# A hand-scheduled section emitted directly instead of in a block with one program per engine

## The chip, the cores and the metric

One core of a Trainium2 chip. The metric is the device time of one execution in microseconds (us). A profiled execution has a "span", from its first to its last recorded instruction, which is about 1.8 us shorter than the device time here. Every run of this study carries the state "fast": its granted clock, a share of full speed that the profile gives, is 1.0. A few of them are nevertheless 40 to 48 us (0.8 to 1.0%) longer than the others of the same kernel. Below they are called outlying runs, and the experiments ended up being largely about them.

## The reference

```python
# x: (256, 256, 4096) float32, eps = 1e-5
mean = np.mean(x, axis=2, keepdims=True)
var = np.var(x, axis=2, keepdims=True)
return ((x - mean) / np.sqrt(var + eps)).astype(np.float32)
```

## The kernel before

The input is taken as 128 tiles of 8.39 MB, each of 128 partitions with four rows of 4096 values. Three tile buffers go round: SyncE (S) loads and stores, VectorE (V) sums and normalises, ScalarE (A) makes the sums of squares and normalises three quarters of one row in four. All synchronisation is by hand, with semaphores: `take` waits for a count and clears the semaphore.

```python
def take(engine, sem, count):
    engine.wait_ge(sem, count)
    engine.sem_clear(sem)

def store(s, t):
    take(S, done[s], K + 1)
    S.dma_start(out=rows_of(out_t, t), in_=X[s][:, :, :]).then_inc(stored[s], 16)

def load(s, t, wait=True):
    if wait:
        take(S, stored[s], 16)
    S.dma_start(out=X[s][:, :, :], in_=rows_of(x_t, t)).then_inc(loaded[s], 16)

with tc.tile_critical():            # the framework adds no synchronisation inside
    with nc.Block() as block:       # a program per engine; a barrier at its end
        @block.sync
        def _(sync):
            ...                     # first loads and stores
            with S.Fori(0, rounds) as i:          # 41 rounds of 3 tiles
                for t in range(L0, L0 + BUFS):
                    store(t % BUFS, (t, BUFS, rounds, i))
                    load((t + 2) % BUFS, (t + 2, BUFS, rounds, i))
            ...                     # last loads and stores, waits for the last stores
        @block.vector
        def _(vector):
            ...
            with V.Fori(0, rounds) as i:
                for j in range(BUFS):
                    vector_tile((L0 + j) % BUFS)
            ...
        @block.scalar
        def _(scalar):
            ...                     # the same with A and scalar_tile
```

## Time and profile before

| kernel before | |
|---|---|
| median of 3 runs | 4962.77 us (4962.52 to 4963.97) |
| span, instructions | 4960.0 us, 5954 |
| data moved, mean rate | 2147.5 MB, 433 GB/s |
| busy: VectorE, ScalarE | 66%, 49% |
| mean time from store to store, 30th to 60th store | 38.638 us |

### The profile page before, as it was taken

What the parts mean: (1) busy time and instruction counts of PE and PEld (TensorE: products, weight loads), DVE (VectorE), ACT (ScalarE), POOL (GpSimd) and SP (SyncE); (2) the same over time, 40 slices, a digit from 0 to 9 for tenths busy, and PEclk for the clock granted to TensorE, in tenths of its full rate; (3) what the DMA queues carried; (4) which work ended last, traced back from release to release, by engine and by line L of the source; (5) the groups of instructions that cost most, each with busy time, mean ns of one, the idle gap of its engine ahead of it and who ended that gap; (6) DMA issues with size and microseconds to landing.
All of it is one profiled execution on the core that took longest, in us unless ns stands there. A gap on an engine that the chain in (4) does not pass through costs nothing.

```text
span 4960.0 us, 5954 instructions
## 1 busy us (share of the span) xinstructions
DVE 3298.0 (66%) x2049; ACT 2407.6 (49%) x1412; POOL 0.2 (0%) x4
## 2 busy tenths in 40 slices
DVE  6666666666666666666666666666666666666666
ACT  4454444554445544455445544455444554445544
POOL 0000000000000000000000000000000000000000
DMA  9999999999999999999999999999999999999999
GB/s 423 431 437 432 431 437 432 432 438 433 434 435 432 435 434 432 436 434 432 436 434 432 437 433 432 438 433 432 438 432 434 435 433 435 434 432 436 434 432 403
DMA packets 37298, 2147.52 MB, mean 433 GB/s; under 512 B 4144, under 2 KB 4144, under 8 KB 4144
## 3 DMA queue, kind: packets, MB, share of 16 engines
q1 hardware_dynamic: 37296, 2147.50, 100.0%
q14 instruction: 2, 0.02, 0.0%
HBM read 1073.74 MB, written 1073.74 MB: 433 GB/s over the span
## 4 chain that ended last, share of the span: by engine, by line
DVE 62%; another core or an unknown queue 31%; issue 4%; DMA 2%; ACT 0%; DVEq 0%; ACTq 0%; SPq 0%
DVE x L87 44%; DVE x L112 17%; DMA x<-in_x_dram 1%; DVE nbias L100 1%; DMA out_dram<-x 1%; DVE rstd L98 1%; ACT junk L137 0%; DVEq L68 0%; DVEq L225 0%; ACT L146 0%; ACT std L146 0%; DVEq L193 0%; ACTq L68 0%; ACTq L67 0%
## 5 line engine op out<-in xcount | busy, mean ns | idle before, releaser
L87 DVE TENSOR_SCALAR_CACHE_REDUCE x<-x 128x4096 f32<-128x4096 f32 x512 | 2232.3, 4416 | 1579.9 <-DMA x<-in_x_dram 1579.9
L137 ACT ACTIVATE junk<-x,mean 128x4096 f32<-128x4096 f32 x512 | 1883.1, 3678 | 2366.7 <-DVE x L87 2366.7
L112 DVE TENSOR_SCALAR x<-x,rstd,nbias 128x4096 f32<-128x4096 f32 (+1 forms) x512 | 1004.2, 2004 | 33.9 <-DVE nbias L100 29.3
L151 ACT ACTIVATE x<-x,nbias,rstd 128x3072 f32<-128x3072 f32 x130 | 383.2, 2948 | 146.2 <-DVEq L68 146.2
L137 ACT ACTIVATION_READ_ACCUMULATOR junk<-x,mean 128x1 f32 x512 | 95.5, 186 | 0.0
L146 ACT ACTIVATE std<-ss,eps_tile 128x2 f32<-128x2 f32 x256 | 75.6, 295 | 19.1
L98 DVE RECIPROCAL rstd<-std 128x2 f32<-128x2 f32 x256 | 40.7, 159 | 19.4 <-ACT std L146 19.4
L100 DVE SCALAR_TENSOR_TENSOR nbias<-mean,rstd 128x2 f32<-128x2 f32 x256 | 41.1, 161 | 8.9
L87 DVE DVE_READ_ACCUMULATOR x<-x 128x1 f32 x512 | 42.4, 83 | 0.0
L137 ACT ACT_TABLE_LOAD x1 | 1.3, 1283 | 1.2 <-DVE eps_tile L222 1.2
L146 ACT ACT_TABLE_LOAD x1 | 1.3, 1283 | 0.1
L222 DVE MEMSET eps_tile<- 128x1 f32 x1 | 0.1, 59 | 1.0 <-SPq L192 1.0
L259 POOL MEMSET const-bfloat16-1.0<- 128x1 bf16 x1 | 0.1, 103 | 0.0
L259 POOL MEMSET const-uint8-127<- 128x1 uint8 x1 | 0.1, 101 | 0.0
L259 POOL MEMSET const-float32-0.0<- 128x1 f32 x1 | 0.1, 99 | 0.2 <-issue 0.2
L259 POOL MEMSET const-float32-1.0<- 128x1 f32 x1 | 0.1, 98 | 0.0
## 6 DMA issues: line engine op xcount, KB each, us to landing
out_dram<-x SPq DMA_DIRECT2D x4, 4096.0 KB, 19.4
x<-in_x_dram SPq DMA_DIRECT2D x2, 4096.0 KB, 16.8
x<-in_x_dram SPq DMA_DIRECT2D x127, 50.3
out_dram<-x SPq DMA_DIRECT2D x126, 31.5
```

Source lines behind the costliest of these rows:

```text
L87: V.tensor_scalar(out=x[:, r, :], in0=x[:, r, :], scalar1=1.0 / d, scalar2=None, op0=ALU.mult, op1=ALU.add, accum_out=mean[s][:, r : r + 1 ...
L98: mine(V.reciprocal(out=rstd[s][:, c], in_=std[s][:, c]))
L100: mine(V.scalar_tensor_tensor(out=nbias[s][:, c], in0=mean[s][:, c], scalar=-1.0 / d, in1=rstd[s][:, c], op0=ALU.mult, op1=ALU.mult))
L112: V.tensor_scalar(out=x[:, r, f], in0=x[:, r, f], scalar1=rstd[s][:, c], scalar2=nbias[s][:, c], op0=ALU.mult, op1=ALU.add,).then_inc(dn, 1)
L137: mine(A.activation(out=junk, in_=x[:, r, :], func=AF.Square, bias=mean[s][:, c], scale=-float(d), accum_out=ss[s][:, c]))
L146: A.activation(out=std[s][:, c], in_=ss[s][:, c], func=AF.Sqrt, bias=eps_tile, scale=1.0 / d**3).then_inc(stds, 1)
L151: A.activation(out=x[:, last, :Q], in_=x[:, last, :Q], func=AF.Identity, bias=nbias[s][:, c], scale=rstd[s][:, c]).then_inc(dn, 1)
L222: V.memset(eps_tile, eps / d**2).then_inc(ready, 1)
L259: nc = _bacc.Bacc("TRN2", target_bir_lowering=False, num_devices=1)
```

## The change

The section keeps its outer frame and loses the block. The calls of the three engines now stand one after another in the source, in the order SyncE, VectorE, ScalarE, and each call goes to its own engine's stream. The intent is to be rid of the block's branches and of its exit barrier. Cut to its core:

```diff
     with tc.tile_critical():
-        with nc.Block() as block:
-
-            @block.sync
-            def _(sync):
-                for h in range(2):
-                    ...
-                with S.Fori(0, rounds) as i:
-                    ...
-            @block.vector
-            def _(vector):
-                V.memset(eps_tile, eps / d**2).then_inc(ready, 1)
-                ...
-            @block.scalar
-            def _(scalar):
-                take(A, ready, 1)
-                ...
+        for h in range(2):
+            ...
+        with S.Fori(0, rounds) as i:
+            ...
+        V.memset(eps_tile, eps / d**2).then_inc(ready, 1)
+        ...
+        take(A, ready, 1)
+        ...
```

(The bodies are the same lines, only less indented.)

More of the change, by code (lines that the diff above doesn't have):

```diff
@@ L192 @@
     with tc.tile_critical():
-        with nc.Block() as block:
-            @block.sync
-            def _(sync):
-                for h in range(2):
-                    r = half_of(h)
-                    S.dma_start(out=X[0][:, r, :], in_=x_t[0][:, r, :]).then_inc(second(loaded, 0, h), 16)
-                load(1, 1, wait=False)
-                store_half(0, 0, 0)
-                store_half(0, 0, 1)
-                load(2, 2, wait=False)
-                store(1, 1)
-                take(S, stored[BUFS], 16)
-                load(0, 3)
-                with S.Fori(0, rounds) as i:
-                    for t in range(L0, L0 + BUFS):
-                        store(t % BUFS, (t, BUFS, rounds, i))
-                        load((t + 2) % BUFS, (t + 2, BUFS, rounds, i))
-                load(last % BUFS, last)
-                store((last - 2) % BUFS, last - 2)
-                store((last - 1) % BUFS, last - 1)
-                store_half(last % BUFS, last, 0)
-                store_half(last % BUFS, last, 1)
-                for s in ((last - 2) % BUFS, (last - 1) % BUFS, last % BUFS, BUFS):
-                    take(S, stored[s], 16)
-            @block.vector
-            def _(vector):
-                V.memset(eps_tile, eps / d**2).then_inc(ready, 1)
-                halves(vector_tile, 0, True)
-                vector_tile(1)
-                with V.Fori(0, rounds) as i:
-                    for j in range(BUFS):
-                        vector_tile((L0 + j) % BUFS)
-                vector_tile((last - 2) % BUFS)
-                vector_tile((last - 1) % BUFS)
-                halves(vector_tile, last % BUFS, False)
-            @block.scalar
-            def _(scalar):
-                take(A, ready, 1)
-                halves(scalar_tile, 0, True)
-                scalar_tile(1)
-                with A.Fori(0, rounds) as i:
-                    for j in range(BUFS):
-                        scalar_tile((L0 + j) % BUFS)
-                scalar_tile((last - 2) % BUFS)
-                scalar_tile((last - 1) % BUFS)
-                halves(scalar_tile, last % BUFS, False)
@@ new lines @@
+        for h in range(2):
+            r = half_of(h)
+            S.dma_start(out=X[0][:, r, :], in_=x_t[0][:, r, :]).then_inc(second(loaded, 0, h), 16)
+        load(1, 1, wait=False)
+        store_half(0, 0, 0)
+        store_half(0, 0, 1)
+        load(2, 2, wait=False)
+        store(1, 1)
+        take(S, stored[BUFS], 16)
+        load(0, 3)
+        with S.Fori(0, rounds) as i:
+            for t in range(L0, L0 + BUFS):
+                store(t % BUFS, (t, BUFS, rounds, i))
+                load((t + 2) % BUFS, (t + 2, BUFS, rounds, i))
@@ new lines @@
+        load(last % BUFS, last)
+        store((last - 2) % BUFS, last - 2)
+        store((last - 1) % BUFS, last - 1)
+        store_half(last % BUFS, last, 0)
+        store_half(last % BUFS, last, 1)
+        for s in ((last - 2) % BUFS, (last - 1) % BUFS, last % BUFS, BUFS):
+            take(S, stored[s], 16)
+        V.memset(eps_tile, eps / d**2).then_inc(ready, 1)
+        halves(vector_tile, 0, True)
+        vector_tile(1)
+        with V.Fori(0, rounds) as i:
+            for j in range(BUFS):
+                vector_tile((L0 + j) % BUFS)
@@ L246 @@
+        vector_tile((last - 2) % BUFS)
+        vector_tile((last - 1) % BUFS)
+        halves(vector_tile, last % BUFS, False)
+        take(A, ready, 1)
+        halves(scalar_tile, 0, True)
+        scalar_tile(1)
+        with A.Fori(0, rounds) as i:
+            for j in range(BUFS):
+                scalar_tile((L0 + j) % BUFS)
+        scalar_tile((last - 2) % BUFS)
+        scalar_tile((last - 1) % BUFS)
+        halves(scalar_tile, last % BUFS, False)
 _INS = ['x', 'eps']
```

## The prediction

The forecast's sum is 0.03 + 0.19 + 0.06 = 0.28 us, from 4962.77 to 4962.5 us.

> **What bounds the kernel now.** I began with the profile's page, to see which resource is full. Its first two parts give the busy shares of the engines and of the 16 DMA engines, slice by slice, and its third part gives the DMA queues (packets, MB, share of the DMA engines' time).
>
> ```profile
> span 4960.0 us, 5954 instructions
> DVE 3298.0 (66%) x2049; ACT 2407.6 (49%) x1412; POOL 0.2 (0%) x4
> ...
> DMA  9999999999999999999999999999999999999999
> ...
> DMA packets 37298, 2147.52 MB, mean 433 GB/s; under 512 B 4144, under 2 KB 4144, under 8 KB 4144
> ...
> q1 hardware_dynamic: 37296, 2147.50, 100.0%
> q14 instruction: 2, 0.02, 0.0%
> ```
>
> The DMA row is full in all 40 slices, while VectorE works two thirds of the time and ScalarE half. The bytes are the input once and the output once (2 x 1073.74 MB), so none can be saved: 2147.52 MB at 433 GB/s is 4960 us, the whole span. The second queue is instruction fetch: two packets in the whole run, which I use below.
>
> A full DMA row says that queues are occupied, not that nothing delays them. So I next read one loop tile in the timeline (start, duration, engine, line, what; idle time and its releaser in brackets).
>
> ```profile
> 2406.69 4.42 DVE L87 TENSOR_SCALAR_CACHE_REDUCE x<-x 128x4096 f32<-128x4096 f32 x1 [12.55 <-DMA x<-in_x_dram]
> ...
> 2433.13 0.34 SPq L165 DMA_DIRECT2D out_dram<-x  x1
> 2433.71 0.35 SPq L170 DMA_DIRECT2D x<-in_x_dram  x1
> 2445.34 4.42 DVE L87 TENSOR_SCALAR_CACHE_REDUCE x<-x 128x4096 f32<-128x4096 f32 x1 [12.45 <-DMA x<-in_x_dram]
> ...
> 2471.64 0.34 SPq L165 DMA_DIRECT2D out_dram<-x  x1
> 2472.22 0.35 SPq L170 DMA_DIRECT2D x<-in_x_dram  x1
> 2483.98 4.42 DVE L87 TENSOR_SCALAR_CACHE_REDUCE x<-x 128x4096 f32<-128x4096 f32 x1 [12.56 <-DMA x<-in_x_dram]
> ```
>
> A tile takes 2483.98 - 2445.34 = 38.64 us. It moves 2 x 8.389 MB = 16.78 MB, which is 434 GB/s. VectorE finishes and then waits about 12.5 us for the next load. When the store is issued at 2433.13, the previous load is still arriving; its first reader starts only at 2445.34. So about 12 us of work lies in the DMA queue when new work is added: SyncE could be that much late before the queue ran dry. A delay of less than that in compute or in issuing, once per tile, should cost nothing.
>
> The change concerns the edges of the program, so I then read who waited for whom on SyncE in the last 10 us (engine, line, releaser: total us, times, longest), and the instructions of the line that opens the block (duration in ns, first and last start in us).
>
> ```profile
> SPq L68 <- DMA out_dram<-x: 9.6, 1, 9.6
> SPq L273 <- PEq L273: 0.5, 2, 0.4
> SPq L193 <- PEq L193: 0.2, 1, 0.2
> ...
> L193 POOLq DRAIN  x1: 41/41/41, 0.9 to 0.9; - x1
> L193 PEldq DRAIN  x1: 8/8/8, 1.0 to 1.0; - x1
> ...
> L193 SPq DRAIN  x1: 7/7/7, 4958.8 to 4958.8; - x1
> L193 SPq EVENT_SEMAPHORE  x1: 17/17/17, 4958.9 to 4958.9; - x1
> ```
>
> The last half store is issued at 4941.19 and lands 17.5 us later, at 4958.7. SyncE clears its semaphore, then enters the block's exit barrier at 4958.8 and leaves it about 0.2 us later; PE's release is the last to come, at 0.2 us. Everything after the last landing takes 4960.0 - 4958.7 = 1.3 us, most of it in barriers that the change does not touch (the section's own exit and the program's two end barriers). PE and POOL wait in the block's exit barrier from the first microsecond on, since they have no program in it; VectorE and ScalarE join it near 4941. Only SyncE's arrival is on the path.
>
> [...] the loops' compare-and-branch has a median of 45 ns on SyncE and 56 ns on VectorE. [...] The trace shows two instruction packets in 4960 us with 41 loop-backs on each of three engines[...]. [...] SyncE's 7 ns drain and 17 ns semaphore in the block's exit span about 0.2 us, so I cost the barrier from start to start and not by adding durations.
>
> **The change part by part.** A comparison of the two built programs, engine by engine and with the semaphores that each waits for, shows that all DMAs, all VectorE and ScalarE instructions, their sizes, order, loops and semaphore counts are the same. The three parts stand one after another in the source, but each engine still gets a stream of its own. What differs is this.
>
> First, each working engine loses its branch from the section into its own program. On SyncE this lies ahead of the first load, but the trace records no instruction for it: from the end of the section's entry branch (0.84 us) to the first load (0.96 us) is 0.12 us in all, so it may already have become a plain fall-through. I take 0.03 us from a possible 0 to 0.1.
>
> Second, the block's exit barrier goes: five drains and six semaphore instructions, which I count in the rows of that line. Only SyncE's passage is on the path: from the drain at about 4958.78 to SyncE's next instruction at about 4958.97, so 0.19 us.
>
> Third, PE and POOL have no work left in the section, so the section's entry and exit no longer include them: two branches with a wait at the start, two drains at the end, and one of SyncE's three semaphore waits (successive ones start about 0.05 us apart). This exit collects the slowest engine, and PE is the last to drain there (about 4959.1); without it I take 0.06 us.
>
> The sum is 0.03 + 0.19 + 0.06 = 0.28 us. The loop, 38.64 us times the tiles, is untouched. From 4962.77 this makes 4962.5 us, or 0.006%. The recorded instructions should fall by 11 + 2 + 2 + 1 = 16, from 5954 to about 5938.
>
> **The rivals.** (a) Another barrier takes over the whole saving: the section's exit still synchronises SyncE, VectorE and ScalarE after the last store. For it speaks that the program's end barrier, too, is released by PE (0.5 us). Against it, barriers here follow each other in series, and PE and POOL will now stand at the end barrier long before SyncE. It would make 4962.8. (b) The loops' code moves[...]. For it: addresses do shift. Against it: the streams only lose a few instructions, two packets were fetched before, and about 12 us per tile would hide such a stall. It would make 4962 to 4964 while hidden[...]. (c) The engines run one part after another, as the source now reads. That would be far slower or would hang, as SyncE's part waits for VectorE's; equal waits and separate streams speak against it. (d) The DMA pace falls differently, because loads and stores overlap at another phase. For it: 1% of pace is 50 us. Against it: every slice is full, and the steady tile repeats to 0.01 us after a start-up that the change does not reorder. (e) The block delayed the start by much more than I think. But the first load goes out at 0.96 us in all, most of it in the program's own preamble, so at most some tenths are to be had: 4962.2.
>
> **Range and chances.** The effect is smaller than the spread of the three runs (4962.52 to 4963.97, 1.45 us). The range has to hold that spread[...]: 4958 to 4967. A change beyond 2% is 99 us, or 0.77 us in each of the 128 tiles after the 12 us of slack is used up[...]. [...] I give 0.5% to faster, 98.5% to same and 1% to slower.
>
> **What would show it.** In the changed profile: the same 434 GB/s and 38.64 us per tile; VectorE still idle about 12.5 us before each tile's first pass; the first load at about 0.93 us; no line of the block, and the stretch from the last store's landing to the end at 1.0 to 1.1 us instead of 1.3; two packets of instruction fetch; about 5938 instructions. I would be wrong if the tile period moved by more than 0.05 us (6 us over the run), if instruction packets multiplied, or if VectorE's wait before a tile shrank because its own stream had slowed.

## The result, and the profile after

The changed kernel took 4961.92 us (median of 6 runs, 4961.67 to 4962.52), the kernel before 4962.85 us in its six (4961.47 to 4963.97). Ratios here are the mean time of one kernel's runs over that of the other's of the same rounds, so not quite the ratio of these medians. The ratio is 0.9998, with a 95% interval of 0.9986 to 1.0011: the same, inside the predicted range.

The page of the changed kernel, to be held against the page lines in the prediction:

```profile
span 4960.2 us, 5938 instructions
DVE 3298.0 (66%) x2049; ACT 2407.7 (49%) x1412; POOL 0.2 (0%) x4
...
DMA packets 37298, 2147.52 MB, mean 433 GB/s; under 512 B 4144, under 2 KB 4144, under 8 KB 4144
...
q14 instruction: 2, 0.02, 0.0%
```

16 instructions fewer, as counted; the compute and the bytes are equal. One loop tile in the timeline of the changed kernel (start, duration, engine, line, what):

```profile
2434.53 0.34 SPq L165 DMA_DIRECT2D out_dram<-x  x1
2435.11 0.35 SPq L170 DMA_DIRECT2D x<-in_x_dram  x1
2446.75 4.42 DVE L87 TENSOR_SCALAR_CACHE_REDUCE x<-x 128x4096 f32<-128x4096 f32 x1 [12.46 <-DMA x<-in_x_dram]
...
2485.37 4.42 DVE L87 TENSOR_SCALAR_CACHE_REDUCE x<-x 128x4096 f32<-128x4096 f32 x1 [12.54 <-DMA x<-in_x_dram]
```

2485.37 - 2446.75 = 38.62 us, and the same 12.5 us of waiting for each load. Store to store, the 30th to the 60th are 38.638 us apart on average, to the digit as before. The loop was not touched.

At the head, the first load in the timeline of before and then of after:

```profile
0.96 0.86 SPq L199 DMA_DIRECT2D x<-in_x_dram  x2
```

```profile
0.96 0.86 SPq L195 DMA_DIRECT2D x<-in_x_dram  x2
```

Nothing was gained there. At the tail, the section's exit sits on the line that opens the section. First SyncE's rows of it in the kernel before (count, durations in ns, first and last start), then in the kernel after:

```profile
L192 SPq EVENT_SEMAPHORE  x3: 17/28/28, 4959.0 to 4959.2; - x3
L192 SPq NOP  x2: 13/13/13, 0.7 to 4959.3; - x2
```

```profile
L192 SPq NOP  x2: 13/13/13, 0.7 to 4959.4; - x2
L192 SPq EVENT_SEMAPHORE  x2: 17/22/28, 4959.2 to 4959.4; - x2
```

The starts, read from the traces' own time stamps to the nanosecond: before, SyncE enters the block's barrier at 4958.756, starts the section's exit at 4958.969, starts the no-operation that closes it at 4959.256, and the span ends at 4960.044. After, the exit starts at 4959.227, its no-operation at 4959.442, and the span ends at 4960.202. So the block's barrier took 0.21 us and is gone, the section's exit went from 0.29 to 0.21 us, and the rest from 0.79 to 0.76 us. From SyncE's first such instruction to the end, 1.29 us became 0.98 us: 0.31 us saved. (Expectation e0 below says 1.24 us, which was worked out with the span rounded to 4960.0.) In these two executions the whole span did not become shorter, because the last half store was issued at 4941.68 instead of 4941.19. This half microsecond is scatter in the loop. Held store against store, the changed kernel is 1.4 us behind from the 31st store on, after another start-up, and wins back 0.9 us late: loads arrive every 38.638 us and then, to the end, every 38.72 us, and this step comes at 4068 us before and at 4494 us after. The step is also in the normal traces with fifty barriers below (at 4146 and 3699 us), and not in that of the second copy; what it comes from is not shown.

### The profile page after: what moved, and what is told of

It reads as the page before. It is cut to its first block, busy times and chain, and to the rows that moved or that the text cites. A ratio compares the mean times of both kernels' runs of the same rounds, so it can differ in the third digit from the quotient of the medians.

```text
span 4960.2 us, 5938 instructions
## 1 busy us (share of the span) xinstructions
DVE 3298.0 (66%) x2049; ACT 2407.7 (49%) x1412; POOL 0.2 (0%) x4
## 4 chain that ended last, share of the span: by engine, by line
DVE 62%; another core or an unknown queue 31%; issue 4%; DMA 2%; ACT 0%; DVEq 0%; ACTq 0%; SPq 0%
DVE x L87 44%; DVE x L112 17%; DMA x<-in_x_dram 1%; DVE nbias L100 1%; DMA out_dram<-x 1%; DVE rstd L98 1%; ACT junk L137 0%; DVEq L68 0%; DVEq L219 0%; ACT L146 0%; ACT std L146 0%; ACTq L68 0%; ACTq L67 0%; SPq L265 0%
## 5 line engine op out<-in xcount | busy, mean ns | idle before, releaser
L98 DVE RECIPROCAL rstd<-std 128x2 f32<-128x2 f32 x256 | 40.7, 159 | 19.4 <-ACT std L146 19.4
```

The source lines that it names most:

```text
L98: mine(V.reciprocal(out=rstd[s][:, c], in_=std[s][:, c]))
```

## The experiments

Twelve kernels ran, in four sets. Every set has its own runs of the kernel before, on the same chip. Where means without outlying runs are given, runs above 4970 us are left out; the unedited ratio is given too.

### The changed kernel again

> The changed kernel once more, in five rounds against the kernel before. My theory (one barrier of about 0.2 us and a thinner section exit of about 0.1 us, both once per run): 0.3 us faster, ratio 0.99994, and the stretch from SyncE's last semaphore clear to the end of the span about 1.0 us instead of 1.24 us. Rival, the block cost nothing on the path: ratio 1.0000 and 1.24 us. Rival, the DMA pace changed with the block: a ratio off by 0.001 or more and another tile period than 38.64 us.

Median 4961.86 us against 4962.31 us; ratio 0.9982, interval 0.9945 to 1.0018. The interval is this wide because one of the 7 runs took 5003.43 us and two of the 11 runs of the kernel before took 5001.73 and 5008.59 us. Without those three, the means are 4961.80 and 4962.17 us, 0.37 us apart; in the first measurement the means were 0.78 us apart. Both have the predicted sign, and neither resolves 0.3 us, as runs of one kernel spread by 2 us. The traces do resolve it. The profiled run was the outlying one, but its tail is the same: 0.975 us from SyncE's first instruction of the section's exit to the end, as in the first trace of the changed kernel. In the eight later traces in which the changed exit stands alone, with extra passes, written-out loops or no computation ahead of it, it is 0.970 to 0.982 us. The 1.29 us of the kernel before come from one trace. The outlying run also gave the first view of the other state:

```profile
1500.00:2400.00 900.00, 595.90 (x369) 433.83 (x255) 0.00 (x0) 1.00 1.00 430
2700.00:3600.00 900.00, 594.82 (x371) 432.44 (x254) 0.00 (x0) 1.00 1.00 429
```

These are stretches of that run (window, its length, busy time with instruction counts of VectorE, ScalarE and GpSimd, clock, DMA share, GB/s). In the same windows the normal run of the changed kernel has:

```profile
1500.00:2400.00 900.00, 599.80 (x374) 436.58 (x257) 0.00 (x0) 1.00 1.00 434
2700.00:3600.00 900.00, 597.55 (x373) 434.35 (x255) 0.00 (x0) 1.00 1.00 434
```

The DMA share is 1.00 in both, and the rate differs by 1%. Store to store, the normal runs of the two kernels settle after some 30 tiles into a pattern of three (38.50, 38.57, 38.84 us; late in the run 38.60, 38.65, 38.92), while the outlying run wanders between 38.5 and 40.2 us (mean 39.08) to its end. I call the first the steady rhythm. Only this one outlying run was profiled; that the others are of the same kind is taken from their times. Both kernels have outlying runs: over all sets 3 of 44 runs before and 1 of 13 after, which says nothing about a difference between them.

### Fifty barriers at the end, and fifty at the start

```diff
         halves(scalar_tile, last % BUFS, False)
+        for _ in range(50):
+            with nc.Block() as block:
+                pass
```

The second kernel has the same three lines as the first statement of the section, ahead of the first load.

> The changed kernel with 50 empty blocks, each with its exit barrier over all engines, behind the last wait of the section: the suspected cost multiplied by 50 at the end. My theory: every barrier there is on the path and costs 0.2 to 0.4 us (0.21 us is what one took in the kernel before; back to back each also waits for PE), so 10 to 20 us longer than the changed kernel. Rival, barriers at the end are absorbed by the program's own end: 0 to 1 us. The loop should be untouched: 434 GB/s and 38.64 us per tile.

> The same 50 empty blocks ahead of the first load instead of at the end. My theory: the first load goes out 10 to 20 us later and the whole run is longer by just that, because a DMA-bound run has no slack that could win back a late start. Rival, the start is hidden (for instance by time that VectorE waits for loads anyway): the run is longer by under 3 us.

At the end: 4979.29 us (ratio 1.0036, interval 0.9990 to 1.0083, one run of 6 outlying at 5026.89). At the start: 4979.23 us (ratio 1.0017, interval 0.9981 to 1.0054, none outlying). Against the changed kernel's 4961.86 us of the same set both are 17.4 us longer, or 0.35 us for each block, inside the expected 10 to 20 us. Both rivals (under 1 us, under 3 us) fall. In the trace with the barriers at the start, the first load goes out at 18.31 us instead of 0.96 us:

```profile
18.31 0.86 SPq L198 DMA_DIRECT2D x<-in_x_dram  x2
```

(18.31 - 0.96) / 50 = 0.347 us. The two views agree, so a block's exit barrier is paid in full on either side, and neither the slack of the loop nor the end of the program takes any of it back. In the two traces 44 and 43 of the 49 steps from one barrier to the next take 0.33 us. Three and four are clearly longer (0.52 to 0.82 us), each within 0.8 us ahead of one of the four more instruction packets that these longer streams fetch, and they add about 1.0 us in all. So the barrier's own price back to back is 0.33 us. That is more than the 0.21 us of the single one in the kernel before. There the four other engines had arrived already (their drains start at 0.91 and 1.05 us on GpSimd and PE and end by 4941.1 us on ScalarE and VectorE, SyncE's starts at 4958.76); here each has to leave one barrier before it can enter the next, and in the trace with the barriers at the start PE is the last that SyncE waits for in 49 of 50:

```profile
SPq L194 <- PEq L194: 13.4, 49, 0.7
```

### More VectorE work per tile

The prediction rests on a slack of about 12 us per tile. To use up a part of it, small passes on a tile of their own (128 x 1024 with a sum) follow each load's wait in the 123 loop tiles: 6, 14, and later 2 of them.

```diff
         if ld:
             take(V, ld, 16)
+        for _ in range(extra):
+            V.tensor_scalar(
+                out=pad, in0=pad, scalar1=1.0, scalar2=None, op0=ALU.mult, op1=ALU.add, accum_out=pad_sum,
+            ).then_inc(pads, 1)
+            take(V, pads, 1)
```

> The changed kernel with 6 extra small VectorE passes (128x1024 with a sum, each waited for) in each of the 123 loop tiles, right after the load's wait; I estimate 1.3 us each from the 4.4 us of a 128x4096 pass, so 8 us per tile on the chain from load to store. My theory (DMA-bound with about 12 us of slack per tile): under 10 us longer over the whole run, tile period still 38.6 us, VectorE's wait for the load down from 12.5 to about 5 us. Rival, the chain load-compute-store-load sets the period and only looks like DMA: 8 us x 123 = 980 us longer.

> The same with 14 extra passes, an estimated 18 us per tile, which is more than the slack. My theory: the slack of 12.5 us is used up and the rest, about 5.5 us, is paid in each of 123 tiles: about 680 us longer, VectorE's wait for loads close to zero and the DMA rate near 434 x 38.6 / 44 = 380 GB/s. Rival, other slack remains (VectorE's own waits inside a tile): under 300 us longer.

> Two extra VectorE passes of 1.22 us per loop tile instead of six, about 2.8 us with their waits. With six, 8.3 us per tile, the run was 68 us longer although VectorE still waited 4.9 us for each load. If the 12 us of slack is free up to a threshold: under 5 us longer. If the DMA pace falls gradually as the queue gets shorter: about a third, 15 to 30 us longer. If any disturbance of the rhythm makes it slip into the slower one of 428 GB/s: about 40 us longer, as in the outlying runs of the kernel before.

| extra passes | time added to the chain per tile | median us | longer than before (means) | ratio, 95% interval |
|---|---|---|---|---|
| 2 | 2.8 us | 5010.22 | 46.9 us (without the outlying run of before) | 1.0080, 1.0042 to 1.0118 |
| 6 | 8.3 us | 5031.28 | 67.6 us | 1.0134, 1.0117 to 1.0151 |
| 14 | 19.4 us | 5788.05 | 824.7 us | 1.1662, 1.1642 to 1.1681 |

(A pass takes 1.385 us from start to start; my estimate of 1.3 us was low, hence 19.4 and not 18 us.) With 14 passes the theory holds: 824.7 / 123 = 6.7 us per tile are paid, so 19.4 - 6.7 = 12.7 us were absorbed, which is the 12.5 us that VectorE used to wait. The rival, under 300 us, falls. But inside the slack the theory fails: 6 passes were to cost under 10 us and cost 68. The wait shows that VectorE was not the limit:

```profile
DVE pad L90 <- DMA x<-in_x_dram: 602.9, 123, 8.5
```

602.9 / 123 = 4.9 us are still spent waiting for each load. The rival that the chain sets the period would have made it about 1000 us, so it falls too. What became slower is the transfers. The stretch from 1500 to 2400 us with 6 passes, then with 2:

```profile
1500.00:2400.00 900.00, 759.40 (x641) 431.10 (x253) 0.00 (x0) 1.00 1.00 427
1500.00:2400.00 900.00, 649.36 (x461) 430.82 (x254) 0.00 (x0) 1.00 1.00 429
```

427 and 429 GB/s at a DMA share of 1.00. The 47 us with 2 passes are nearest to the third of the three readings laid down for it: not a gradual third of 68 us, but the size of the outlying runs. It is not one slower rhythm with one price either, since 6 passes cost 68. None of the 4 runs with 2 passes and none of the 4 with 6 was as fast as a normal run. A pass both delays the store and adds work of VectorE; no run has the delay alone. That VectorE's work as such slows the transfers is made unlikely by the second copy below, which has none of it and is only 3 us faster.

### The transfers alone

Both kernels copy the input to the output, a wrong result. The first issues each load only once its own buffer's store has landed:

```diff
+        for t in range(3):
+            load(t, t, wait=False)
+        with S.Fori(0, rounds) as i:
+            for t in range(BUFS):
+                put(t, (t, BUFS, rounds, i))       # waits for loaded[t], then stores
+                load(t, (t + 3, BUFS, rounds, i))
```

The second has the kernel's order:

```diff
+                put(t % BUFS, (t, BUFS, rounds, i))
+                load((t + 2) % BUFS, (t + 2, BUFS, rounds, i))
```

> The same loads and stores in the same three buffers with no computation at all (a wrong result on purpose: it copies the input). It shows the floor that the transfers alone set. My theory: the same 434 GB/s, so 2147.5 MB take 4948 us and the run 4945 to 4960 us, at most 0.3% under the changed kernel. Rival, the compute engines slow the transfers or the handshakes leave holes in the queue: below 4900 us.

> The copy without computation again (wrong result on purpose), now in the kernel's own order: each store as soon as its load has landed, and a load behind each store of the tile before[...]. The first copy took 5457 us because its queue ran dry once per tile. My theory (transfers alone set the pace when the queue never runs dry): 430 to 435 GB/s and 4940 to 5010 us. Rival (transfers of this kind are slower whatever the order, unless compute spaces them): above 5100 us again.

The first took 5456.74 us (ratio 1.0992, interval 1.0974 to 1.1011), which neither side had foreseen. It is my flaw: in SyncE's stream the wait for a store's landing stands ahead of the next load, so the queue can empty before that load is issued. The page shows the gaps, a queue at 95.1%, and shows also how coarse the DMA row is, for all 40 slices read 9:

```profile
DMA  9999999999999999999999999999999999999999
...
q1 hardware_dynamic: 36864, 2147.50, 95.1%
```

A queue at 95.1% instead of 100.0% is 268 us of the 5456.6 us span. The other 230 or so of the 497 us by which the span is longer than before's is in a lower rate while transfers run. The second copy took 4959.13 us (4957.96 to 4960.32; ratio 0.9985, interval 0.9948 to 1.0022, wide for the one outlying run of before). It is in the steady rhythm in the trace, with 100.0% on the queue:

```profile
q1 hardware_dynamic: 36864, 2147.50, 100.0%
```

So these transfers in this order, with no computation on the tiles, take only about 3 us (0.06%) less than either kernel. This is not a lower bound for every version: another order, or a start-up that settles sooner, was not tried.

### Loops written out

The loops are replaced by Python loops, so that the programs hold no branch and all 123 tiles' instructions.

```diff
-        with V.Fori(0, rounds) as i:
-            for j in range(BUFS):
-                vector_tile((L0 + j) % BUFS)
+        for j in range(BUFS * rounds):
+            vector_tile((L0 + j) % BUFS)
```

and likewise for ScalarE and SyncE, first for all three, then for SyncE alone, then for VectorE and ScalarE alone.

> The changed kernel with its three loops written out over all 123 tiles, so that there is no branch in them and the instruction streams are some tens of times longer. My theory (code layout and branches are not on the path): within 1 us of the changed kernel, while the packets of the instruction queue rise from 2 to some tens. Rival, instruction fetch or branches matter: a few us faster if the 41 loop-backs cost time, or 10 us and more slower if fetches get in the way of the data transfers or stall an engine for longer than the 12 us of slack per tile.

> Only SyncE's loop written out; VectorE and ScalarE keep theirs. It splits the 20 to 47 us that the fully written-out kernel was longer, with a DMA rate of 428 instead of 434 GB/s. Theory A (instruction fetches disturb the rhythm of loads and stores): few fetches here, under 10 packets, so the time stays at 4962 us and the tile period at 38.64 us in most runs. Theory B (the DMA instructions with fixed addresses are issued closer together, 0.44 us instead of 0.58 us from store to load, and that shifts the rhythm): all runs 20 to 47 us longer here.

> Only the loops of VectorE and ScalarE written out; SyncE keeps its loop. Theory A (instruction fetches disturb): some 30 packets of instruction fetch and 20 to 47 us longer in all or most runs. Theory B (SyncE's closer issues): as the changed kernel, 4962 us in most runs.

| written out | instruction packets | median us (range) | ratio, 95% interval |
|---|---|---|---|
| none (changed kernel) | 2 | 4961.86 (4960.71 to 4962.92, and 5003.43) | 0.9982, 0.9945 to 1.0018 |
| SyncE | 6 | 4967.26 (4964.91 to 4975.62) | 1.0003, 0.9974 to 1.0031 |
| VectorE, ScalarE | 36 | 4996.22 (4986.91 to 5012.65) | 1.0055, 1.0025 to 1.0085 |
| all three | 40 | 4992.76 (4982.39 to 5009.53) | 1.0044, 1.0004 to 1.0083 |

My theory for the first of them, no difference within 1 us, fell: all runs were 20 to 48 us longer. Of the two readings for the split, B (closer issues by SyncE) falls, as SyncE alone brings 5 us in the median and the other two engines bring the whole effect. A (instruction fetches) fits in order of size but not exactly, since it had SyncE alone at 4962 us, and all six of its runs were 3 to 14 us longer. Nor is the effect of a single fetch plain. In the profiled run of SyncE alone the steady rhythm lived through the fetches between 1900 and 1950 us and between 3150 and 3200 us, and broke near 4060 us, with the next fetch after 4400 us.

### Fetches by an engine that has nothing else to do

Writing loops out also changes the engines' own streams. Here those stay, and GpSimd, which touches no data in the section, gets a long stream of waits.

```diff
             for t in range(L0, L0 + BUFS):
                 store(t % BUFS, (t, BUFS, rounds, i))
                 load((t + 2) % BUFS, (t + 2, BUFS, rounds, i))
+                S.sem_inc(tick, 1)
...
+        G = nc.gpsimd
+        for t in range(BUFS * rounds):
+            G.wait_ge(tick, t + 1)
+            for _ in range(160):
+                G.wait_ge(tick, t + 1)
```

> The changed kernel with a long stream of waits on GpSimd, which has nothing else to do and touches no data: about 160 wait instructions for each loop tile of the second half of the run (the built program starts them at the 62nd of 123 loop tiles), so that its instructions have to be fetched there, while the streams and loops of SyncE, VectorE and ScalarE stay as they are but for one semaphore increment per tile. Theory A (instruction fetches beside the data transfers break the rhythm): tile period 38.64 us in the first half, wandering and about 39.1 us in the second, some 20 to 30 us longer in most runs, and some 30 packets on the instruction queue in the second half. Rival (what slowed the kernel with written-out VectorE and ScalarE loops lies in those engines' own streams): 4962 us in most runs and 38.64 us in both halves.

All 5 runs took 5004.11 to 5009.12 us (ratio 1.0085, interval 1.0071 to 1.0098; none of the 9 runs of before was outlying). The built program, as expected, leaves GpSimd without anything to fetch until the 62nd loop tile (its first wait is recorded at 2472.8 us), so one run holds both cases. The DMA view of two stretches of 900 us, first from 1500, then from 2700 us:

```profile
DMA packets 6700, 390.86 MB, mean 434 GB/s; under 512 B 736, under 2 KB 736, under 8 KB 736
...
q1 hardware_dynamic: 6700, 390.86, 100.2%
```

```profile
DMA packets 6644, 385.59 MB, mean 428 GB/s; under 512 B 735, under 2 KB 735, under 8 KB 735
...
q1 hardware_dynamic: 6615, 385.35, 99.9%
q14 instruction: 29, 0.24, 0.1%
```

And SyncE's stores in the timeline around the first fetches (the first packet falls between 2400 and 2500 us, then about three in each 100 us):

```profile
2549.23 0.34 SPq L166 DMA_DIRECT2D out_dram<-x  x1
...
2587.74 0.34 SPq L166 DMA_DIRECT2D out_dram<-x  x1
...
2626.55 0.34 SPq L166 DMA_DIRECT2D out_dram<-x  x1
...
2666.07 0.34 SPq L166 DMA_DIRECT2D out_dram<-x  x1
...
2705.12 0.34 SPq L166 DMA_DIRECT2D out_dram<-x  x1
...
2745.06 0.34 SPq L166 DMA_DIRECT2D out_dram<-x  x1
```

The differences are 38.51, 38.81, 39.52, 39.05, 39.94 us. From the 30th to the 60th store the mean is 38.64 us, from the 70th to the 124th 39.46 us, and the steady pattern does not come back. This is more than theory A had said (39.1 us and 20 to 30 us longer), and the rival (4962 us) falls. The bytes fetched, 0.65 MB over the run, would take 1.5 us by my estimate from the measured 434 GB/s; the run is 43 us longer (5005.99 against 4963.23 in the means), or 0.56 us for each of the 77 packets more. The added semaphore increment is not the cause, for it is in the first half too.

In the second half GpSimd also executes the waits, in bursts of 161 for each tile (43 ns each, one in 87 ns), and the experiment alone does not tell them from the fetches. The trace does so in part. A tile's burst always has 161 waits, but the packets come five in four tiles, so that one tile in four has two of them. Counted from one load's arrival to the next (start of VectorE's first pass), from 2561 to 4850 us, the 43 tiles with one packet take 39.22 us in the mean (38.96 to 39.49), the 16 with two 40.05 us (38.90 to 40.51, all but the first over 39.8). So the period follows the packets while the number of waits stays the same. The first two packets, and the first three tiles with waits, left the period at 38.64 us. In the written-out kernels, which have no such bursts, the difference is smaller and the ranges overlap: the tiles with one packet take 39.28 us against 38.95 without (all three written out) and 39.27 against 39.03 (VectorE and ScalarE), from 200 us on.

## Why the prediction was right or wrong

**The time and the mechanism were right.** 4962.5 us were predicted, 4961.9 us came. With runs that spread by 2 us, this agreement could not have told the forecast from no effect; what supports the mechanism is the tail in the traces. The sum of 0.28 us for the tail and head stands against 0.31 us there. Its terms:

- The branch ahead of the first load, 0.03 us: measured 0.00, the first load starts at 0.96 us in both. As the prediction suspected, there was no such instruction to remove.
- The block's exit barrier, 0.19 us: 0.21 us from start to start.
- PE and GpSimd leaving the section's exit, 0.06 us: 0.07 us (0.287 to 0.215 us; two successive semaphore waits of SyncE's start 0.064 us apart there). A last 0.03 us, behind the exit, was not in the sum.
- "The recorded instructions should fall by 16": they fell by 16, and two packets of instruction fetch stayed two.

That such a barrier is paid in full was put to the test with fifty of them: 17.4 us, at either end. The gain is small because the barrier is paid once per run, and one run is 128 tiles of 38.64 us.

**The claim of free slack was wrong.** The prediction says of a delay under about 12 us, once per tile, that it "should cost nothing". 2.8 us per tile cost 47 us and 8.3 us cost 68 us. The slack is real in the sense that the chain becomes the limit only beyond 12.7 us. But the prediction took the DMA pace for a constant because the row was full and "the steady tile repeats to 0.01 us". It is a rhythm of loads and stores that settles after some 30 tiles at 434 GB/s, and small extra passes keep it at 427 to 429 GB/s. Even undisturbed it is not constant: the loads' period steps from 38.64 to 38.72 us in the very trace that the prediction reads, at 4068 us, where it did not look. This touches neither the number nor the range, since the change adds no delay in the loop.

**Rivals (b) and (d) were dismissed for the wrong reason.** Rival (b) was to be hidden by the slack. The kernels with fetches in the loop took 5 us (4 packets more), 31 to 34 us (38 and 34 more) and 43 us (77 more) longer, with slower transfers and the DMA share still full. It was not what the prediction pictured with "such a stall", an engine that stalls for longer than the slack: VectorE in the written-out kernels still waited 1628 and 1635 us in all for its loads, 1580 us in the changed kernel. The kernel before and the changed one fetch two packets in the whole run and stay clear of it. Against (d), "every slice is full" is no argument: at 428 GB/s every slice is full as well. What did hold is that the change itself did not move the pace: 38.638 us in the normal profiled runs of both kernels.

**The record of a branch is not the whole of its time.** The prediction quotes the loop's compare-and-branch with the 45 ns of its record on SyncE (56 ns on VectorE). SyncE's next instruction, a register move, starts 164 ns after the start of the branch (median of 41, in both traces). It is as with the barrier, where records of 7 and 17 ns stand in a passage of 0.21 us. Nothing in the sum rests on it.

**What stays open.** Why 3 of 44 runs of the kernel before and 1 of 13 of the changed one were outlying, without added delays or fetches. Why the loads' period steps to 38.72 us late in normal runs. And what inside the DMA engines makes the same packets, at 99.9 to 100% busy, take 1 to 2% longer off the rhythm. That extra passes set it off is shown by every run that has them. For fetches it is shown that kernels which fetch are slower, and in one trace that the period follows the packets; that a fetch alone does it was not isolated. The mechanism is not shown for either. Whether the change alters the frequency of outlying runs cannot be told from these counts.

## What to carry to other kernels

An all-engine barrier outside the loop took 0.21 us here when the others waited already and 0.33 us back to back, and fifty of them were paid in full (17.4 us) although VectorE waited 12.5 us for each load in the loop; count how often it runs before you spend effort on it. A DMA row of nines tells that transfers are under way, not that they run at their best: here it went with 434 GB/s (steady), 426 to 430 (off the rhythm) and 394 (a copy whose queue was busy 95.1% of the time). Read the GB/s and the time from store to store, and look at the queue's share of time. In a kernel whose DMA share is 1.00 like this one, prefer a loop that fetches no instructions, since all kernels here that fetched in the loop were slower (by 5 us with 4 packets more, by 31 to 43 us with 34 to 77 more), and do not take a wait for a load as time that may be spent freely: 2.8 us of it cost 47 us over the run.
